# Residual additions and the gates' offset by accumulating DMAs, and the gates' sigmoids three steps later, in a streaming-encoder block on one core

## The chip, the cores and the metric

The kernel runs on one core of a Trainium2 chip. The time is the device time of one execution in microseconds (us); three runs of the kernel before gave a median of 2434.71 us (2432.69 to 2434.84). The core has five engines that each work through their own list of instructions in order: TensorE (PE, with PEld for its weight loads), VectorE (DVE), ScalarE (ACT), GpSimd (POOL) and SyncE (SP), which here issues nearly all DMAs. An engine that comes to an instruction whose inputs are not there waits, and everything behind it in its list waits too.

## The reference

One encoder block on 256 tokens of width 2048, everything in float32: two feed-forward parts with a mixer and a cross attention between them, each added to the scaled residual stream and normalised.

```python
ALPHA = 2.0 ** 0.25
def swiglu_ffn(x, w_in, w_out):                 # width 5504
    g, u = jnp.split(x @ w_in, 2, axis=-1)
    return (jax.nn.silu(g) * u) @ w_out
def hybrid_mixer(u, ...):
    proj = u @ w_in
    qa, ka, va, q_lat, kv_lat, gates = jnp.split(proj, ...)
    y_a = chunked_relbias_attention(...) @ w_o_a
    y_b = mla_attention(...) @ w_o_b
    g = jax.nn.sigmoid(gates + gate_bias)       # 256 x 4096
    g_a, g_b = jnp.split(g, 2, axis=-1)
    return (g_a * y_a + g_b * y_b) @ w_out
h = layer_norm(ALPHA * h + 0.5 * swiglu_ffn(h, ffn1...))
h = layer_norm(ALPHA * h + hybrid_mixer(h, ...))
h = layer_norm(ALPHA * h + memory_cross_attention(h, mem, ...))
h = layer_norm(ALPHA * h + 0.5 * swiglu_ffn(h, ffn2...))
```

## The kernel before

**Weights and the split.** All products have a float32 accuracy that is made of two parts of each operand: a high part hi and a remainder lo. The weights come from memory in chunks of 1 MB (a tile *raw* of 128 x 2048, three buffers), loaded by SyncE (L193), one chunk after the other through the whole kernel. ScalarE copies a chunk into *hi* in two pieces of 128 x 1024 (L264), VectorE subtracts hi from raw and writes *lo* (L267, one instruction of 128 x 2048). TensorE multiplies hi·hi, hi·lo and lo·hi. A chunk covers two blocks of 128 of the inner dimension, for 256 tokens by 1024 output columns: 24 matmuls of 512 columns (`mm_pair`, L311).

**Sums chunks.** For some chunks the product is formed from seven products instead of eight: VectorE makes sums of the weights (`weight_sums`, L248 one instruction of 128 x 1024 and L250 two of 128 x 512) in a tile such as *H*, these are split like a weight (*X* in the rows below), and `mm_sums` (L366) does 21 matmuls. A part of the results is gathered in four PSUM tiles of its own. After the last sums chunk `shared` brings them together: ScalarE copies two (L679, L680), VectorE does four additions (L681 to L684), and the four 128 x 512 tiles in SBUF, `qs["add"]`, in buffers called *w* (six of that kind), hold what is still to be added to the plain product.

**The items.** The program is written as a list of items, about one per chunk (`add`). `collect` builds such a list apart, and `weave` puts side work before given items of it, with a priority. Loads run ahead of the items. A scheduler then makes each engine's list from the order and priorities, so an instruction's place on its engine is not its place in the code.

**Output pairs.** `out_pair` makes 1024 output columns of the residual stream *h* (four tiles of 128 x 512 in two tiles for the tokens). After `shared` its inner function adds `qs["add"]` to h on VectorE: with the factor ALPHA where the pair is the first to touch these columns (L629), else plainly (L631). When all chunks are done, `finish` (L754) adds the PSUM tiles, and the last pairs also feed the statistics of the normalisation (L390). Seven pairs have sums chunks: two and one in each feed-forward part, and one in the cross attention's output (xo). Two pairs of the mixer's output have none, and only use `finish` with the factor.

**Gates.** Four gate groups follow each other, each 1024 columns: `product` adds the four tiles of `qs["add"]` to PSUM (L921), adds the bias (L923), which GpSimd has loaded as a row repeated over the partitions into tile X1 (L912, 512 KB), and takes the sigmoid on ScalarE (L924, two of 128 x 1024 a gate). It is scheduled soon after the gate's last chunk. The results are used only after the attention.

Of the kernel before, what the change touches and what calls it, by code (L numbers as in the profile page):

```python
# [14 lines left out]
ALU = mybir.AluOpType  # L15
# [3 lines left out]
P = 128  # L19
S = 256  # L20
D = 2048
KT = D // P
# [5 lines left out]
SUMS_IN = {2: ("X0", 0), 4: ("X0", 1), 6: None}  # L28
# [3 lines left out]
SUMS_GATE, AT_GATE = {**SUMS_IN, 5: ("F", 0)}, ((2, 4, 5, 6), (2, 4, 5, 6), (2, 4, 6), (2, 4, 6))  # L32
ORDER_GATE = (0, 2, 1, 4, 5, 3, 6, 7)
# [8 lines left out]
SUM_HOME = ("X2", "X3"),  # L42
# [5 lines left out]
ALPHA = 2.0 ** 0.25  # L48
# [53 lines left out]
class Kernel:  # L102
# [513 lines left out]
            turn = None  # L616
            f0 += nf

    def out_pair(self, bank, src, g, nk, x, at, fx, scale, st, sums_in=SUM_HOME):

        nc, h = self.nc, self.h
        ps, qs = {}, {}

        def shared():
            for (tt, a), s in qs["add"].items():
                c = (2 * g + a) * 512
                hs = h[tt][:, c:c + 512]
                if scale:
                    nc.vector.scalar_tensor_tensor(hs, hs, ALPHA, s, ALU.mult, ALU.add)  # L629
                else:  # L630
                    nc.vector.tensor_tensor(hs, hs, s, ALU.add)  # L631

        def finish():
            for tt in range(2):
                for a in range(2):
                    self.finish(tt, 2 * g + a, ps[tt, a], scale and not at, st)
        self.pair_group(bank, src, 512, nk, x, at, fx, ps, qs, shared, sums_in)
        self.add(finish)

    def group_tile(self, j):  # L640
# [229 lines left out]
    def mixer(self, xT, st, steps):  # L870
        nc, t = self.nc, self.t
# [24 lines left out]
        ps = {}  # L896
# [3 lines left out]
        a, b, c = steps(1)  # L900
        self.weave(first, {0: a, 3: b, 4: c})
        gates, fx = {}, {}
# [1 line left out]
        self.weave(second, {1 + i: [self.forms_step(fx, SUMS_GATE, c, xT)] for i, c in enumerate(SUMS_GATE)}, prio=0)  # L904


        bias = {}

        def load_bias(n):
            if "t" not in bias:  # L910
                bias["t"] = self.block("X1", (P, 2, 1024))
            nc.gpsimd.dma_start(bias["t"][:, n % 2, :], t["gate_row"][n:n + 1, :].to_broadcast([P, 1024]))  # L912

        def gate(n):
            ps, qs = {}, {}

            def product():
                g = gates[n] = self.block(f"H{n}", (P, 2, 2, 512))
                for tt in range(2):
                    for a in range(2):  # L920
                        nc.vector.tensor_tensor(g[:, tt, a, :], qs["add"][tt, a], ps[tt, a], ALU.add)  # L921
                    v = g[:, tt].rearrange("p a n -> p (a n)")
                    nc.vector.tensor_tensor(v, v, bias["t"][:, n % 2, :], ALU.add)  # L923
                    nc.scalar.activation(v, v, AF.Sigmoid)  # L924
                if n < 2:
                    load_bias(n + 2)
            self.pair_group(n % 2, t["w_gate"][n], 512, KT, xT, AT_GATE[n], fx, ps, qs, None, SUM_HOME + ("H5",),
                            ORDER_GATE if len(AT_GATE[n]) > 3 else None)
            self.add(product, prio=SOON)

        self.add(lambda: [load_bias(n) for n in range(2)])
        for n in range(4):
            gate(n)


        lps, lqs = {}, {}
# [25 lines left out]
        def lat_send(k):  # L962
            def fn():
                for tt in range(2):
                    with self.tc.issue_after(self.last_load.ins):
                        self.sent = self.send(self.lat[:, tt, k, :], self.lu[:, k, tt, :], 512)
            return fn

        def lat_join(k):
            def fn():  # L970
                if k == 0:
                    self.c = self.act(["X0", "X2"])
                for tt in range(2):
                    self.join(self.lat[:, tt, k, :], self.lu[:, k, tt, :], 512)
                v = self.lu[:, k].rearrange("p t (j c) -> p t j c", j=4)
                for j in range(4):
                    gain = self.vec(("q_a_norm", "kv_a_norm")[k], j)
                    hi, lo = (self.c.at(half, 4 * k + j).rearrange("p (t c) -> p t c", t=2) for half in (0, 1))
                    nc.scalar.mul(hi, v[:, :, j, :], gain)
                    nc.vector.scalar_tensor_tensor(lo, v[:, :, j, :], gain, hi.bitcast(F32), ALU.mult, ALU.subtract)  # L980
            return fn

        self.pair_group(0, t["w_lat"][0], 512, KT, xT, SUMS_IN, fx, lps, lqs, None, SUM_HOME + ("H5",))
        self.add(lat_scale, prio=SOON)
        self.add(lat_planes)

# [225 lines left out]
        for i in range(NA):  # L1212
            side = [[lat_send(0)], [], [lat_join(0)], [lat_join(1)]][2 * i:2 * i + 2] if i < 2 else ([], [])
# [21 lines left out]
        for h in range(B_HEADS):  # L1235
# [18 lines left out]
            if h in (2, 5, 8, 11):  # L1254
                self.add(lambda q=h // 3: self.gb_apply(0, self.h, (q,)), held=held, prio=LATE)
        n = B_HEADS - 1
        ends = {1: [b_out(n - 3), b_send(n), b_out(n - 2)],
                2: [b_join(n - 1), b_out(n - 1)],
                3: [lambda: setattr(self, "early", False), b_join(n), b_out(n)]}
# [52 lines left out]
        main = self.collect(lambda: out_a(0))  # L1312
# [4 lines left out]
        side = out_b(0)  # L1317
        last = {}
        main = self.collect(lambda: last.update(out_b(1)))
# [5 lines left out]
        side = self.mem_norm()  # L1325
# [451 lines left out]
```

## Time and profile before

| | |
|---|---|
| runs | 2434.71 us median (2432.69 to 2434.84) |
| profiled execution | 2432.52 us |
| its span | 2430.7 us |
| DMA engines, mean rate | 212 GB/s |

The prediction shows the profile's rows beside its steps. Three kinds are used. The page's busy line gives each engine's time, its share of the span and its number of instructions. Windows give the same for a stretch of the span. Rows of the chain or of single lines have a start and a duration in us, the engine, the line, the operation, the tile written `<-` the tiles read, the shape, a count where several stand together, and in brackets the idle time before the instruction with what ended it.

### The profile page before, as it was taken

Reading aid. Unit: us, or ns where it says so; the run is one execution under the profiler, and the core shown is the slowest. Engines: PE = TensorE matmul, PEld = TensorE weight load, DVE = VectorE, ACT = ScalarE, POOL = GpSimd, SP = SyncE. Lnnn points to the kernel's source line nnn. Section 1 sums busy time; section 2 is a strip of 40 time slices with the busy share of each in tenths; the row PEclk is TensorE's granted clock in tenths of the full one; section 3 lists DMA queues with packets and bytes.
Section 4 is the critical chain, followed back from the end, with each engine's and each line's share of the span. In section 5 each row is a group of like instructions: output and inputs, shape, how many; then the busy total and the mean of one; then the engine's idle time right before and its main releaser. Section 6 shows DMA issues by size and latency. Waiting matters only on the chain.

```text
span 2430.7 us, 29702 instructions
## 1 busy us (share of the span) xinstructions
PE 2422.3 (100%) x11280; PEld 2022.8 (83%) x11280; DVE 2130.9 (88%) x2437; ACT 1553.2 (64%) x2022; POOL 35.9 (1%) x81
## 2 busy tenths in 40 slices
PE   9999999999999999999999999999999999999999
PEld 8888888888888888888888888888888888888887
DVE  8999989899889998779788889979879999888997
ACT  6676745666555557878565687765666675556662
POOL 0000000000000001000000000000000000000000
PEclk9999999999999999999999999999999999999999
DMA  7766656667656657776577577655556766666665
GB/s 268 252 212 214 207 200 222 210 201 219 224 176 215 216 195 248 229 210 176 183 246 256 167 241 213 220 181 192 190 199 214 229 221 210 220 207 207 200 220 182
DMA packets 176414, 516.20 MB, mean 212 GB/s; under 512 B 111728, under 2 KB 112496, under 8 KB 121104
## 3 DMA queue, kind: packets, MB, share of 16 engines
q1 hardware_dynamic: 170816, 495.83, 61.6%
q0 software_dynamic: 4592, 17.30, 2.2%
q8 instruction: 88, 1.44, 0.2%
q10 hardware_dynamic: 864, 1.18, 0.1%
q14 instruction: 54, 0.44, 0.1%
HBM read 485.30 MB, written 2.10 MB: 201 GB/s over the span
## 4 chain that ended last, share of the span: by engine, by line
PE 89%; DVE 4%; ACT 3%; DMA 1%; issue 1%; SPq 0%; DVEq 0%; ACTq 0%
PE at L311 24%; PE mm L311 23%; PE at L366 11%; PE mm L366 11%; PE mm L298 10%; PE mm L277 4%; PE mm L279 2%; DVE lo L267 2%; ACT hi L264 1%; PE at L1034 1%; PE at L1505 0%; PE at L277 0%; DMA raw<-w_xv 0%; PE at L1088 0%; ACT H L854 0%
## 5 line engine op out<-in xcount | busy, mean ns | idle before, releaser
L264 ACT CAST hi<-raw 128x1024 fp32r<-128x1024 f32 (+1 forms) x852 | 804.0, 981 | 458.0 <-PE at L311 150.1
L267 DVE TENSOR_TENSOR lo<-raw,hi 128x2048 fp32r<-128x2048 f32 (+1 forms) x427 | 902.0, 2114 | 134.8 <-ACT hi L264 129.0
L311 PE MATMUL mm<-hi,T 128*128 128x512 f32 (+1 forms) x1312 | 307.5, 384 | 0.8 <-DVE v L400 0.7
L311 PEld LDWEIGHTS mm<-hi,T 128*128 128x128 f32 x1312 | 244.5, 188 | 46.9 <-DVE v L400 1.1
L264 ACT CAST X<-H 128x1024 fp32r<-128x1024 f32 (+1 forms) x170 | 174.8, 1035 | 160.9 <-DVE H L248 119.9
L311 PE MATMUL at<-hi,T 128*128 128x512 f32 x1136 | 272.3, 390 | 0.0
L311 PEld LDWEIGHTS at<-hi,T 128*128 128x128 f32 x1136 | 213.3, 188 | 44.5
L267 DVE TENSOR_TENSOR X<-H,X 128x2048 fp32r<-128x2048 f32 (+1 forms) x85 | 191.4, 2252 | 64.7 <-ACT X L264 64.7
L311 PE MATMUL mm<-lo,T 128*128 128x512 f32 (+1 forms) x656 | 158.4, 383 | 0.0
L311 PE MATMUL at<-lo,T 128*128 128x512 f32 x568 | 141.0, 389 | 0.0
L311 PEld LDWEIGHTS mm<-lo,T 128*128 128x128 f32 x656 | 122.3, 188 | 22.4
L311 PE MATMUL at<-hi,H 128*128 128x512 f32 x560 | 133.8, 390 | 0.0
L311 PEld LDWEIGHTS at<-lo,T 128*128 128x128 f32 x568 | 106.7, 188 | 22.1
L311 PEld LDWEIGHTS at<-hi,H 128*128 128x128 f32 x560 | 105.0, 188 | 21.5
L250 DVE TENSOR_TENSOR H<-H,raw 128x512 f32<-128x512 f32 (+1 forms) x170 | 115.4, 679 | 2.2
L311 PE MATMUL mm<-hi,H 128*128 128x512 f32 x480 | 115.5, 392 | 0.1
L311 PEld LDWEIGHTS mm<-hi,H 128*128 128x128 f32 x480 | 89.6, 188 | 18.9 <-DVE w L684 0.5
L248 DVE TENSOR_TENSOR H<-raw 128x1024 f32<-128x1024 f32 (+1 forms) x85 | 102.1, 1201 | 0.6 <-DMA raw<-w_gate 0.4
L366 PE MATMUL mm<-X,X 128*128 128x512 f32 x342 | 91.4, 393 | 0.0
L264 ACT CAST X<-raw 128x1024 fp32r<-128x1024 f32 (+1 forms) x54 | 55.4, 1035 | 47.9 <-DVE raw L250 38.6
L366 PE MATMUL at<-X,X 128*128 128x512 f32 (+1 forms) x315 | 82.6, 386 | 0.7 <-ACT X L264 0.7
L854 ACT COPY w<-w 128x1024 uint16<-128x1024 uint16 (+1 forms) x60 | 75.7, 1275 | 1.4 <-DMA w<-w 1.4
(387 smaller groups left out, 4151.3 us busy)
## 6 DMA issues: line engine op xcount, KB each, us to landing
raw<-ffn_w_in SPq DMA_DIRECT2D x150, 1024.0 KB, 4.9
raw<-ffn_w_out SPq DMA_DIRECT2D x66, 1024.0 KB, 4.9
raw<-w_gate SPq DMA_DIRECT2D x32, 1024.0 KB, 4.8
raw<-ffn_w_out_r SPq DMA_DIRECT2D x16, 1024.0 KB, 4.9
raw<-w_qk SPq DMA_DIRECT2D x16, 1024.0 KB, 5.6
raw<-w_o_b SPq DMA_DIRECT2D x16, 1024.0 KB, 4.8
raw<-w_out SPq DMA_DIRECT2D x16, 1024.0 KB, 5.0
raw<-w_xk SPq DMA_DIRECT2D x16, 1024.0 KB, 5.4
```

The costliest lines, as they stand in the source:

```text
L248: self.nc.vector.tensor_tensor(two[0], two[1], raw[:, :m].unsqueeze(1).to_broadcast([P, 2, m]), ALU.add)
L250: self.nc.vector.tensor_tensor(t[:, a * m:a * m + m], t[:, b * m:b * m + m], raw[:, a * m:a * m + m], ALU.add)
L264: self.last_hi = self.nc.scalar.copy(hi[:, c:d], src[:, c:d])
L267: self.last_lo = self.nc.vector.tensor_tensor(lo[:, :n], src, hi[:, :n].bitcast(F32), ALU.subtract)
L277: self.nc.tensor.matmul(ps, hi[j], x.both(kt), start=(j == 0), stop=False)
L279: self.last_mm = self.nc.tensor.matmul(ps[:, :S], lo[j], x.at(0, kt), start=False, stop=(j == n - 1))
L298: self.last_mm = self.nc.tensor.matmul(ps, x.at(xi, kt)[:, tt * P:(tt + 1) * P], w[wi][:, j * 512 + c:j * 512 + c + m], start=(start and j ...
L311: self.last_mm = self.nc.tensor.matmul(ps[tt, g][:, :n], x.at(xi, kt)[:, tt * P:(tt + 1) * P], w[wi][:, c:c + n], start=first and j + wi + ...
L366: self.last_mm = self.nc.tensor.matmul(bank[:, :m], a[xi], v[wi][:, c * m:(c + 1) * m], start=own and first and wi + xi == 0, stop=own and ...
L854: self.nc.scalar.copy(self.words(u, n).rearrange("p (c k) -> p k c", k=2), self.words(s, n).rearrange("p (k c) -> p k c", k=2))
L1034: nc.tensor.matmul(ps[:, c0:c0 + nk], q[:, tt * P:(tt + 1) * P], k[:, :nk], start=(j == 0), stop=(j == len(parts) - 1))
```

## The change

Three edits. In `out_pair` the additions of `qs["add"]` to h become 28 DMAs on GpSimd's queue, 256 KB each, that add to their destination (`accum_op=ALU.add`). Where h needs the factor ALPHA, two ScalarE multiplications of 128 x 1024 (`scaled`) do that beforehand, put in as side work before the third item of the pair. In the gates the bias tile, its four loads and the eight additions go, and eight accumulating DMAs of 512 KB add the bias row, repeated over the partitions, from memory to the gate. The sigmoids become a function of their own, put in as side work before the fourth item of the group that follows (the latents' group for the last gate). Lines behind the edits move by up to three.

```diff
--- before.py
+++ after.py
@@ -616,25 +616,27 @@
             turn = None
             f0 += nf
 
-    def out_pair(self, bank, src, g, nk, x, at, fx, scale, st, sums_in=SUM_HOME):
+    def out_pair(self, bank, src, g, nk, x, at, fx, scale, st, sums_in=SUM_HOME, order=None):
 
         nc, h = self.nc, self.h
         ps, qs = {}, {}
+
+        def scaled():
+            for tt in range(2):
+                hs = h[tt][:, g * 1024:(g + 1) * 1024]
+                nc.scalar.mul(hs, hs, ALPHA)
 
         def shared():
             for (tt, a), s in qs["add"].items():
                 c = (2 * g + a) * 512
-                hs = h[tt][:, c:c + 512]
-                if scale:
-                    nc.vector.scalar_tensor_tensor(hs, hs, ALPHA, s, ALU.mult, ALU.add)
-                else:
-                    nc.vector.tensor_tensor(hs, hs, s, ALU.add)
+                nc.gpsimd.dma_start(h[tt][:, c:c + 512], s, accum_op=ALU.add)
 
         def finish():
             for tt in range(2):
                 for a in range(2):
                     self.finish(tt, 2 * g + a, ps[tt, a], scale and not at, st)
-        self.pair_group(bank, src, 512, nk, x, at, fx, ps, qs, shared, sums_in)
+        main = self.collect(lambda: self.pair_group(bank, src, 512, nk, x, at, fx, ps, qs, shared, sums_in, order))
+        self.weave(main, {2: [scaled]} if scale and at else {}, prio=0)
         self.add(finish)
 
     def group_tile(self, j):
@@ -904,14 +906,7 @@
         self.weave(second, {1 + i: [self.forms_step(fx, SUMS_GATE, c, xT)] for i, c in enumerate(SUMS_GATE)}, prio=0)
 
 
-        bias = {}
-
-        def load_bias(n):
-            if "t" not in bias:
-                bias["t"] = self.block("X1", (P, 2, 1024))
-            nc.gpsimd.dma_start(bias["t"][:, n % 2, :], t["gate_row"][n:n + 1, :].to_broadcast([P, 1024]))
-
-        def gate(n):
+        def gate(n, side):
             ps, qs = {}, {}
 
             def product():
@@ -920,17 +915,22 @@
                     for a in range(2):
                         nc.vector.tensor_tensor(g[:, tt, a, :], qs["add"][tt, a], ps[tt, a], ALU.add)
                     v = g[:, tt].rearrange("p a n -> p (a n)")
-                    nc.vector.tensor_tensor(v, v, bias["t"][:, n % 2, :], ALU.add)
+                    nc.gpsimd.dma_start(v, t["gate_row"][n:n + 1, :].to_broadcast([P, 1024]), accum_op=ALU.add)
+
+            def ends():
+                for tt in range(2):
+                    v = gates[n][:, tt].rearrange("p a n -> p (a n)")
                     nc.scalar.activation(v, v, AF.Sigmoid)
-                if n < 2:
-                    load_bias(n + 2)
-            self.pair_group(n % 2, t["w_gate"][n], 512, KT, xT, AT_GATE[n], fx, ps, qs, None, SUM_HOME + ("H5",),
-                            ORDER_GATE if len(AT_GATE[n]) > 3 else None)
+            main = self.collect(lambda: self.pair_group(
+                n % 2, t["w_gate"][n], 512, KT, xT, AT_GATE[n], fx, ps, qs, None, SUM_HOME + ("H5",),
+                ORDER_GATE if len(AT_GATE[n]) > 3 else None))
+            self.weave(main, side, prio=0)
             self.add(product, prio=SOON)
-
-        self.add(lambda: [load_bias(n) for n in range(2)])
+            return {3: [ends]}
+
+        side = {}
         for n in range(4):
-            gate(n)
+            side = gate(n, side)
 
 
         lps, lqs = {}, {}
@@ -980,7 +980,9 @@
                     nc.vector.scalar_tensor_tensor(lo, v[:, :, j, :], gain, hi.bitcast(F32), ALU.mult, ALU.subtract)
             return fn
 
-        self.pair_group(0, t["w_lat"][0], 512, KT, xT, SUMS_IN, fx, lps, lqs, None, SUM_HOME + ("H5",))
+        main = self.collect(lambda: self.pair_group(
+            0, t["w_lat"][0], 512, KT, xT, SUMS_IN, fx, lps, lqs, None, SUM_HOME + ("H5",)))
+        self.weave(main, side, prio=0)
         self.add(lat_scale, prio=SOON)
         self.add(lat_planes)
 
```

The changes of order at three places follow. The first is ScalarE at the end of gate 1 and the start of gate 2. H_933 (before) and H_932 (after) are gate 1's tile, H_932 and H_931 the tile of gate 2's weight sums, X_940 and X_939 their hi, hi_6209 and hi_6206 the hi of the sums chunk's raw weights, hi_6245 and hi_6242 that of the chunk after. Before:

```order
L680 COPY w_925_6125<-mm_5926 128x512
L264 CAST hi_6160<-raw_6158 128x1024 x2
L264 CAST hi_6209<-raw_6165 128x1024
L924 ACTIVATE H_933_6171<-H_933_6171 128x1024
L264 CAST hi_6209<-raw_6165 128x512
L924 ACTIVATE H_933_6171<-H_933_6171 128x1024
L264 CAST hi_6245<-raw_6243 128x1024
L264 CAST X_940_6214<-H_932_6167 128x1024
L264 CAST hi_6245<-raw_6243 128x1024
```

and of the changed kernel:

```order
L682 COPY w_924_6125<-mm_5924 128x512
L264 CAST hi_6160<-raw_6158 128x1024 x2
L264 CAST X_939_6211<-H_931_6167 128x1024
L264 CAST hi_6206<-raw_6165 128x1024
L264 CAST hi_6206<-raw_6165 128x512
L923 ACTIVATE H_932_6171<-H_932_6171 128x1024 x2
L264 CAST X_939_6211<-H_931_6167 128x1024
L264 CAST hi_6242<-raw_6240 128x1024 x2
```

The two sigmoids now stand together, behind the raw hi and the first half of the sums' hi, and ahead of its second half.

The second place is VectorE in the same stretch: L921 and L923 before, L916 after, write the gate. Before:

```order
L681 TENSOR_TENSOR w_926_6126<-w_924_6124,mm_5927 128x512
L682 TENSOR_TENSOR w_925_6125<-w_925_6125,w_926_6126 128x512
L921 TENSOR_TENSOR H_933_6171<-w_924_6124,at_5884 128x512
L683 TENSOR_TENSOR w_926_6126<-w_926_6126,mm_5928 128x512
L684 TENSOR_TENSOR w_927_6127<-w_925_6125,mm_5928 128x512
L921 TENSOR_TENSOR H_933_6171<-w_925_6125,at_5885 128x512
L921 TENSOR_TENSOR H_933_6171<-w_926_6126,at_5886 128x512
L923 TENSOR_TENSOR H_933_6171<-H_933_6171,X_836_5581 128x1024
L921 TENSOR_TENSOR H_933_6171<-w_927_6127,at_5887 128x512
L267 TENSOR_TENSOR lo_6161<-raw_6158,hi_6160 128x2048
L923 TENSOR_TENSOR H_933_6171<-H_933_6171,X_836_5581 128x1024
L248 TENSOR_TENSOR H_932_6167<-raw_6165 128x1024
```

and of the changed kernel:

```order
L683 TENSOR_TENSOR w_925_6126<-w_923_6124,mm_5925 128x512
L684 TENSOR_TENSOR w_924_6125<-w_924_6125,w_925_6126 128x512
L248 TENSOR_TENSOR H_931_6167<-raw_6165 128x1024
L685 TENSOR_TENSOR w_925_6126<-w_925_6126,mm_5926 128x512
L686 TENSOR_TENSOR w_926_6127<-w_924_6125,mm_5926 128x512
L916 TENSOR_TENSOR H_932_6171<-w_923_6124,at_5882 128x512
L916 TENSOR_TENSOR H_932_6171<-w_924_6125,at_5883 128x512
L916 TENSOR_TENSOR H_932_6171<-w_925_6126,at_5884 128x512
L916 TENSOR_TENSOR H_932_6171<-w_926_6127,at_5885 128x512
L267 TENSOR_TENSOR lo_6161<-raw_6158,hi_6160 128x2048
L250 TENSOR_TENSOR H_931_6167<-H_931_6167,raw_6165 128x512
L267 TENSOR_TENSOR lo_6207<-raw_6165,hi_6206 128x1536
```

The two bias additions are gone, and the first instruction of the next weight sums has moved ahead of the last two additions of `shared` and of the gate.

The third place is VectorE at the end of xo's pair; h_101 and h_102 are the residual stream's two tiles. Before:

```order
L684 TENSOR_TENSOR w_2117_13688<-w_2115_13686,mm_13517 128x512
L629 SCALAR_TENSOR_TENSOR h_101<-h_101,w_2115_13686 128x512
L629 SCALAR_TENSOR_TENSOR h_102<-h_102,w_2116_13687 128x512
L629 SCALAR_TENSOR_TENSOR h_102<-h_102,w_2117_13688 128x512
L267 TENSOR_TENSOR lo_13726<-raw_13723,hi_13725 128x2048
L754 TENSOR_TENSOR h_101<-h_101,at_13336 128x512
L754 TENSOR_TENSOR h_101<-h_101,at_13337 128x512
L390 BN_STATS bn_13731<-h_101 128x6 x2
L754 TENSOR_TENSOR h_102<-h_102,at_13338 128x512
L754 TENSOR_TENSOR h_102<-h_102,at_13339 128x512
```

and of the changed kernel:

```order
L686 TENSOR_TENSOR w_2116_13689<-w_2114_13687,mm_13518 128x512
L756 TENSOR_TENSOR h_101<-h_101,at_13335 128x512
L390 BN_STATS bn_13732<-h_101 128x6
L267 TENSOR_TENSOR lo_13727<-raw_13724,hi_13726 128x2048
L756 TENSOR_TENSOR h_101<-h_101,at_13336 128x512
L756 TENSOR_TENSOR h_102<-h_102,at_13337 128x512
L390 BN_STATS bn_13732<-h_101 128x6
L390 BN_STATS bn_13737<-h_102 128x6
L756 TENSOR_TENSOR h_102<-h_102,at_13338 128x512
L390 BN_STATS bn_13737<-h_102 128x6
```

`finish` (now L756) stands right behind the last addition of `shared`, its first addition ahead of the lo.

## The prediction

> **What bounds the kernel now.** I read the page's busy line and its chain first, then the windows by stage, and then single instructions on either side of the edits.
>
> ```profile
> PE 2422.3 (100%) x11280; PEld 2022.8 (83%) x11280; DVE 2130.9 (88%) x2437; ACT 1553.2 (64%) x2022; POOL 35.9 (1%) x81
> PE 89%; DVE 4%; ACT 3%; DMA 1%; issue 1%; SPq 0%; DVEq 0%; ACTq 0%
> ```
>
> The span is 2430.7 us, so TensorE is without a matmul for 8.4 us in all. A busy PE need not be a fast one, so the rate has to be looked at too, in an undisturbed stretch of the chain and in the stages that the change touches (windows: span, then busy time and count of PE, PEld, DVE, ACT, POOL, clock, DMA share, GB/s):
>
> ```profile
> 1330.12 43.55 PE at L311 x192
> 257.00:319.00 62.00, 62.00 (x276) 51.36 (x275) 57.56 (x58) 38.28 (x45) 0.00 (x0) 1.00 0.65 215
> 740.00:937.00 197.00, 196.97 (x864) 161.43 (x863) 178.41 (x144) 114.71 (x128) 2.50 (x4) 1.00 0.60 208
> 1640.00:1697.00 57.00, 57.00 (x274) 47.77 (x274) 55.20 (x71) 35.68 (x51) 0.00 (x0) 1.00 0.57 202
> 2369.00:2431.00 62.00, 57.28 (x251) 45.52 (x249) 44.51 (x65) 17.58 (x20) 1.27 (x1) 0.98 0.51 178
> ```
>
> 192 matmuls of 512 columns in 43.55 us are 226.8 ns each. The first out pair (257 to 319) runs 276 in 62.00 us, 224.6 ns; the gates (740 to 937) 864 in 197 us, 228.0 ns, which is 864 x 1.2 ns = 1.0 us over the undisturbed rate. In the xo pair PE is never idle. Of the 8.4 idle microseconds 4.7 are behind the last matmul (62.00 - 57.28), where the change has nothing. **So PE is full exactly where VectorE is to be relieved, and about 1 us is all that can be won there.** The question of this case is whether the new waits reach PE.
>
> **What is taken away.**
>
> ```profile
> L629 DVE SCALAR_TENSOR_TENSOR h<-h,w x20: 682/684/693, 307.2 to 2115.0; 128x512 f32<-128x512 f32 x20
> L631 DVE TENSOR_TENSOR h<-h,w x8: 683/685/686, 624.7 to 2366.4; 128x512 f32<-128x512 f32 x8
> L923 DVE TENSOR_TENSOR H<-H,X x8: 1219/1222/1225, 772.3 to 900.9; 128x1024 f32<-128x1024 f32 x8
> L924 ACT ACTIVATE H<-H x8: 1052/1062/1065, 773.6 to 902.1; 128x1024 f32<-128x1024 f32 x8
> ```
>
> VectorE loses 20 x 0.684 + 8 x 0.685 + 8 x 1.222 = 28.9 us of 2130.9. All of it lies beside matmuls, so I credit the path with 0.3 us, a third of the 1.0 us found in the gates, with bounds 0 and 1.0. ScalarE gains 10 multiplications of 128x1024 at the 1.06 us of its sigmoids, 10.6 us. They cost nothing as long as an early hi covers them: in the first pair ScalarE is busy 38.28 of 62 us and, as the rows below show, its hi is 5 us ahead of PE; without that cover each costs at most its 1.06 us. GpSimd gets 36 issues for 4; it is 1% busy, and no product waits for its other work there.
>
> **What is added: waits for landings.** No accumulating DMA stands in this trace. The nearest rows are GpSimd's own loads of the same sizes: 256 KB (gb) and the 512 KB of the very same gate row, with issue to landing as minimum, median and maximum behind them.
>
> ```profile
> w<-gb POOLq DMA_DIRECT2D x24, 256.0 KB, 4.2
> X<-gate_row POOLq DMA_DIRECT2D x4, 512.0 KB, 5.8
> DMA to landing us min/median/max: 3.3/4.2/8.8
> DMA to landing us min/median/max: 5.4/5.8/6.4
> ```
>
> An accumulating DMA also reads its destination. I bound its landing by 3.3 us below and by twice the gate row's median, 11.6 us, above. I take 6.5 us for the 512 KB ones, just over the same-size row's maximum, and 5 us for the 256 KB ones.
>
> The Trainium skill, page "DMA: Bandwidth & Descriptors", section "Anatomy of one DMA — SWDGE (gpsimd) path", gives 2.0 us plus bytes over 436 GB/s, an estimate of 3.2 us for 512 KB. The 5.8 us row is well over that, so the row is used; by the page's figure no sigmoid would wait long enough to matter and the sum would be the 0.3 us credit alone.
>
> **The gates.** The order of ScalarE shows that a sigmoid, although put three steps later in the code, moves past a row or two of hi only. Gate 1 is the tightest. VectorE, ScalarE and PE there, before:
>
> ```profile
> 808.39 2.29 DVE L267 TENSOR_TENSOR lo<-raw,hi 128x2048 fp32r<-128x2048 f32 x1
> 813.78 1.28 DVE L921 TENSOR_TENSOR H<-w,at 128x512 f32<-128x512 f32 x2
> 822.85 1.42 DVE L250 TENSOR_TENSOR H<-H,raw 128x512 f32<-128x512 f32 x2
> 824.46 2.29 DVE L267 TENSOR_TENSOR lo<-raw,hi 128x2048 fp32r<-128x2048 f32 x1 [0.20 <-ACT hi L264]
> 815.99 1.06 ACT L264 CAST hi<-raw 128x1024 fp32r<-128x1024 f32 x1 [3.22 <-PE mm L311]
> 820.16 1.06 ACT L924 ACTIVATE H<-H 128x1024 f32<-128x1024 f32 x1 [1.65 <-DVE H L923]
> 825.56 1.04 ACT L264 CAST X<-H 128x1024 fp32r<-128x1024 f32 x1
> 825.08 1.07 PE L366 MATMUL at<-X,X 128*128 128x512 f32 x4
> ```
>
> In the new order VectorE goes on at 810.6 (end of the lo at 808.39) with two adds of shared, the 1.2 us first half of the sums, two more adds and four L921. Counted at 0.63 us an add (half of the 1.28) the first half of the gate is ready at 815.6 and the second at 816.9; the sums' last part follows by 822. Landing L later, ScalarE does both sigmoids (1.0 us each) and only then the second half of the sums' hi (X, 1.0), and VectorE its lo (2.2). PE begins the sums at 825.08 and, by its new order, wants that second half four matmuls later, at 826.0, and the lo after eight, at 826.9. The second landing is at 816.9 + L, the sigmoid ends 1.0 later, X 1.0 later, lo 2.2 later: 821.1 + L. **PE loses L - 5.8 us.** What queues behind a waiting sigmoid is thus hi, lo, and PE in turn. In gates 2 and 3 the X stands between the two sigmoids, so only the first landing counts (1.3 us earlier): PE loses L - 7.1 us each. Gate 0 has a whole chunk more in front and begins to lose at about 10.5 us. At 6.5 us that is 0.7 + 0 + 0 + 0 = 0.7 us; at 5.8 nothing; at 8.8, 3.0 + 2 x 1.7 = 6.4; at 11.6, 5.8 + 2 x 4.5 + 1.1 = 15.9.
>
> **The out pairs.** finish (L754) now waits for landings instead of following the additions. VectorE and PE in the first pair of ffn1, and in the pair of xo, where only one chunk lies between:
>
> ```profile
> 312.52 0.68 DVE L684 TENSOR_TENSOR w<-w,at 128x512 f32<-128x512 f32 x1
> 318.71 1.28 DVE L754 TENSOR_TENSOR h<-h,mm 128x512 f32<-128x512 f32 x2 [1.51 <-PE mm L311]
> 328.26 1.98 PE L311 MATMUL at<-lo,H 128*128 128x512 f32 x8
> 305.68 1.05 ACT L264 CAST hi<-raw 128x1024 fp32r<-128x1024 f32 x1 [1.69 <-DMA raw<-ffn_w_out]
> 312.14 2.00 ACT L264 CAST hi<-raw 128x1024 fp32r<-128x1024 f32 x2 [3.50 <-PE mm L311]
> 319.19 3.79 PE L311 MATMUL at<-hi,H 128*128 128x512 f32 x16
> 1694.28 0.69 DVE L682 TENSOR_TENSOR w<-w,w 128x512 f32<-128x512 f32 x1
> 1695.61 0.68 DVE L684 TENSOR_TENSOR w<-w,mm 128x512 f32<-128x512 f32 x1
> 1704.99 2.27 DVE L267 TENSOR_TENSOR lo<-raw,hi 128x2048 fp32r<-128x2048 f32 x1
> 1709.58 1.07 PE L298 MATMUL mm<-lo,X 128*128 128x512 f32 x4
> ```
>
> In ffn1 the last sum is ready at 313.2 and finish comes at 318.7, 5.5 us later; what stands behind it is a lo that PE wants at 328.26, so landings up to some 12 us cost PE nothing. The second pair's finish is later still, and ffn2 repeats both. In xo the last sum is ready at about 1695.7 (0.6 earlier without the addition at its head); the four additions (2.5 us) are gone, but the fourth finish waits for 1695.7 + L. At 5 us that is 1700.7, before VectorE gets there, and the lo of 1704.99 comes no later than now. At 8.8 us it ends at about 1709.1, still ahead of 1709.58; at 11.6 PE loses some 2 us.
>
> **Sum.** -0.3 + 0.7 + 0 = +0.4 us on the profiled 2432.52 (span 2430.7 and 1.8 around it), 2432.9. The median of the runs shown, 2434.71, is 2.2 above that execution, so the forecast is 2432.9 + 2.2 = 2435.1 us, no change that can be told. A measurement of this kernel can tell about 0.2%, 4.9 us, from none.
>
> **Rivals.**
> 1. *Slow landings.* If the accumulation makes a 512 KB landing 8.8 to 11.6 us, the sigmoids hold ScalarE, and the sums above give 6.4 to 15.9 + 2 = 17.9 us more; at 10 us it is 4.2 + 2 x 2.9 = 10.0 in place of 0.7, giving 2444.4. It decides against the forecast from L = 8.4, where the gates' 2.6 + 2 x 1.3 = 5.2 us pass 4.9. For it: nothing in this trace adds to a destination, and gb had one landing of 8.8. Against it: the gate row's four lie within 5.4 to 6.4. Chance 17%.
> 2. *The accumulations crowd the weight loads.* In the first pair the DMA engines are 0.65 busy for 215 GB/s, 331 at full share. Four DMAs of 256 KB with their destinations read are 2.1 MB, 6.3 us of all engines in one burst. The hi at 305.68 already waited 1.69 us for its load, so a late load is a late hi; that of 312.14 ends 5.1 us before PE wants it at 319.19. A load 6.3 us late would cost 1.2 us in each of seven pairs, 8.4 us: 2443.5. Against it: two thirds of the engines' time is taken, one third free, and the burst is spread over 6 us by VectorE. The Trainium skill, same page, section "Issuing engines are not separate DMA queues", speaks against the change here: GpSimd's transfers run on the same engines as SP's. That the engines are shared the trace can show only for loads: theirs spread as the row below has it, with no accumulation among them. Chance 5%.
>
> ```profile
> DMA to landing us min/median/max: 3.4/4.9/9.7
> ```
>
> 3. *VectorE's relief reaches PE elsewhere.* The order of many chunks shifts a little; if waits outside these stages went, 3.7 us of idle PE before the tail (8.4 - 4.7) and 1 us of slow rate would be the most: 2435.1 - 4.7 = 2430.4. Chance 5%, and hardly beyond 0.2%.
> 4. *The change does not do what it says.* The scaling is hoisted to ffn1's third group and the sigmoids move by a row or two: the landing wait is then the whole effect, which is the forecast's 0.7 us or rival 1.
>
> **How the numbers follow.** The forecast, landings up to 7.5 us, has 73%. The range runs from 2431.5 (credit 1.0, no loss, and a median 2 us lower by chance) to 2446, which takes in rival 2 and most of rival 1; some 8% lie above and 6% below. Faster by over 0.2%: 4%, the end of rival 3. Slower: rival 1's 17% and most of rival 2, 21%. Same: 75%.
>
> **What would show it.** PE at 100% and 226.8 ns in the same stages, with VectorE down by about 29 us and ScalarE up by 10.6, shows the first step. Landings of the new DMAs near 6.5 and 5 us, ScalarE waiting for them at the sigmoids by a few microseconds with no hole on PE at the sums' chunks of gates 1 to 3, shows the second; holes there of L - 5.8 would show the sum right and the landing wrong. A finish that waits for a DMA while lo arrives in time shows the third. I am wrong if PE gets holes at the out pairs, if the weight loads land later there, or if the time falls by more than 5 us.

## The result and the profile after

The changed kernel took 2446.45 us in the median (2444.79 to 2451.94, 5 runs), the kernel before 2434.84 us (2432.69 to 2435.88, 5 runs) on the same chip: 11.6 us more, a ratio of 1.0053 with a 95% interval of 1.0042 to 1.0064. The forecast was 2435.1 us with a range up to 2446, so the time lies 0.45 us above the range.

The busy line and the chain of the changed kernel's page:

```profile
PE 2426.3 (99%) x11280; PEld 2021.7 (83%) x11280; DVE 2107.3 (86%) x2401; ACT 1561.1 (64%) x2032; POOL 65.1 (3%) x113
PE 75%; issue 8%; DVE 7%; DMA 4%; ACT 4%; SPq 0%; POOL 0%; DVEq 0%; ACTq 0%; POOLq 0%
```

VectorE is busy for 23.6 us less (2130.9 to 2107.3; the removed instructions were 28.9), ScalarE for 7.9 us more, and neither helps TensorE: the span grew by 15.7 us (2430.7 to 2446.4), and TensorE, which was idle for 8.4 us, now is for 20.1. VectorE, DMAs and ScalarE have come into the chain. Two stages hold most of the new idle time, the gates and the second half of the cross attention's output. The windows of these two stages in the changed kernel (span, then busy time and count of PE, PEld, DVE, ACT, POOL, clock, DMA share, GB/s):

```profile
741.00:944.00 203.00, 198.60 (x867) 161.71 (x866) 170.43 (x136) 115.11 (x128) 8.41 (x10) 1.00 0.67 220
1640.00:1760.00 120.00, 117.17 (x537) 96.74 (x536) 102.30 (x125) 69.37 (x92) 3.53 (x4) 0.99 0.63 213
```

TensorE stands for 203.00 - 198.60 = 4.4 us at the gates and for 2.8 us around the xo pair, where it stood for 0.03 and 0 before. The holes are not the whole loss at the gates: it did 867 matmuls in these 203 us, the kernel before 890, and 23 matmuls are 5.2 us at 0.227 each. What it waits for is seen in the order of time. ScalarE at the end of gate 1 in the changed kernel (start, duration, instruction, idle time before it and its releaser), and behind it TensorE:

```profile
819.04 1.57 ACT L264 CAST hi<-raw 128x1024 fp32r<-128x1024 f32 x2 [2.52 <-issue]
822.10 1.06 ACT L923 ACTIVATE H<-H 128x1024 f32<-128x1024 f32 x1 [1.49 <-DMA H<-gate_row]
828.36 1.06 ACT L923 ACTIVATE H<-H 128x1024 f32<-128x1024 f32 x1 [5.20 <-DMA H<-gate_row]
829.32 1.03 ACT L264 CAST X<-H 128x1024 fp32r<-128x1024 f32 x1
...
828.09 1.07 PE L366 MATMUL at<-X,X 128*128 128x512 f32 x4
830.40 0.74 PE L366 MATMUL at<-X,X 128*128 128x512 f32 x2 [1.25 <-ACT X L264]
...
832.73 0.96 PE L366 MATMUL at<-X,X 128*128 128x512 f32 x3 [1.11 <-DVE X L267]
```

This is the chain that the prediction's gate paragraph worked out, link by link: the second sigmoid waits 5.20 us for its landing, the second half of the sums' hi (X) starts only behind it at 829.32, TensorE wants it after four matmuls and waits 1.25 us, and then 1.11 us more for VectorE's lo of the same sums. What differs is the landing. The DMAs of this gate, and of all four gates, issue to landing:

```profile
L918 POOL DMA_DIRECT2D H<-gate_row x2: 863/864/866, 817.2 to 818.4; - x2
DMA to landing us min/median/max: 4.8/7.4/9.9
...
L918 POOL DMA_DIRECT2D H<-gate_row x8: 863/863/871, 773.9 to 906.5; - x8
DMA to landing us min/median/max: 4.8/7.5/9.9
```

The first accumulation of a gate lands after 4.8 to 5.2 us, the second, issued 1.2 us later, after 9.8 to 9.9, in every gate. The forecast had 6.5 us for each.

The changed kernel's profiled execution (2448.21 us) is 1.8 us above its median, and that of before 2.3 below, which is why the two spans lie 15.7 us apart and the medians 11.6. A part of that is a wait for weight loads ahead of the normalisation behind the first feed-forward part, where TensorE's hole was 1.6 us in this profile; in those of the experiments below it lay between nothing and 2.6 us (0.8 in E7, whose pairs have no DMAs), so it is not counted.

### The profile page after: what moved, and what is told of

Its sections match the earlier page's. It is cut to its first block, busy times and chain, and to the rows that moved or that the text cites. A ratio compares the mean times of both kernels' runs of the same rounds, so it can differ in the third digit from the quotient of the medians.

```text
span 2446.4 us, 29787 instructions
## 1 busy us (share of the span) xinstructions
PE 2426.3 (99%) x11280; PEld 2021.7 (83%) x11280; DVE 2107.3 (86%) x2401; ACT 1561.1 (64%) x2032; POOL 65.1 (3%) x113
## 3 DMA queue, kind: packets, MB, share of 16 engines
q0 software_dynamic: 9200, 26.74, 4.6%
## 4 chain that ended last, share of the span: by engine, by line
PE 75%; issue 8%; DVE 7%; DMA 4%; ACT 4%; SPq 0%; POOL 0%; DVEq 0%; ACTq 0%; POOLq 0%
PE at L311 23%; PE mm L311 20%; PE mm L366 9%; PE at L366 9%; PE mm L298 5%; PE mm L277 4%; DVE lo L267 3%; PE mm L279 2%; ACT hi L264 2%; PE at L1036 1%; DMA raw<-w_xq 1%; ACT X L264 1%; DMA raw<-w_gate 1%; PE at L1507 0%; PE at L277 0%
## 5 line engine op out<-in xcount | busy, mean ns | idle before, releaser
L366 PEld LDWEIGHTS mm<-X,X 128*128 128x128 f32 x342 | 63.7, 188 | 15.1 <-DVE X L267 2.1
```

The source lines that it names most:

```text
L366: self.last_mm = self.nc.tensor.matmul(bank[:, :m], a[xi], v[wi][:, c * m:(c + 1) * m], start=own and first and wi + xi == 0, stop=own and ...
```

## The experiments

All ratios are to the kernel before on the same chip in the same series.

### Which part costs

E1 has the change in the gates alone (`out_pair` as before), E2 in the output pairs alone (gates as before). The diff of each is the corresponding part of the change's diff.

> Only the gates' part of the change; the output pairs add on VectorE as before. Theory A (the landings: ScalarE stands at the second sigmoid of a gate until the second 512 KB accumulation lands about 10 us after its issue, and the hi behind it is late for TensorE): the gates lose what the trace of the changed kernel shows there, 4.4 us of idle TensorE between 740 and 937, so about 2439.5 us, and nothing is lost at the xo pair or at the normalisation behind it. Theory B (the accumulations crowd the weight loads): the gates carry 4 of the 11 MB that are added, so about a third of the 11.6 us, 2438.5, and it shows as late weight loads, not as waits for the gate row. Theory C (only the instructions' new order costs): the same 2439 but no wait of ScalarE for a landing before TensorE's holes.

> Only the output pairs' part; the gates as before. Theory A: the additions of finish wait for the 256 KB landings (8 us in the changed kernel); in ffn1 and ffn2 something else covers that, in xo the lo behind them is late, a weight buffer comes free late, and 3 to 4.5 us are lost at the normalisation behind xo: 2438 to 2440 us. Theory B: each of the seven pairs loses a part, and the time is 2441 to 2443, the holes spread over ffn1 and ffn2 too.

E1 took 2441.70 us against 2433.82 (ratio 1.0034, 1.0021 to 1.0046), 7.9 us more; E2 2438.56 (1.0023, 1.0013 to 1.0032), 4.7 us more. Together that is 12.6 us, about the whole loss of 11.6. Windows of E1 and of E2 over the gates and the xo pair:

```profile
741.00:940.00 199.00, 191.85 (x832) 156.58 (x831) 164.45 (x129) 109.40 (x122) 7.14 (x8) 0.99 0.65 211
1640.00:1760.00 120.00, 120.00 (x561) 100.07 (x560) 108.61 (x140) 71.28 (x94) 0.00 (x0) 1.00 0.58 204
```

```profile
741.00:940.00 199.00, 198.97 (x872) 162.83 (x871) 181.49 (x147) 116.82 (x134) 3.72 (x9) 1.00 0.60 210
1640.00:1760.00 120.00, 115.87 (x543) 96.00 (x542) 101.64 (x134) 67.27 (x91) 3.52 (x4) 1.00 0.60 202
```

With the gates' part alone TensorE stands for 7.2 us at the gates and not at all at xo; with the pairs' part alone it is full at the gates and stands for 4.1 us at xo. Theory A had the places right and the gates' size too low (2439.5 expected); the second landing was 11.6 us at gate 1 in this run. Theory B's holes at all seven pairs are not there.

### The landing, the place, or the traffic at the gates

E3 adds the bias on VectorE again, from the loaded tile, and keeps the sigmoids as side work three steps later:

```diff
-                    nc.gpsimd.dma_start(v, t["gate_row"][n:n + 1, :].to_broadcast([P, 1024]), accum_op=ALU.add)
+                    nc.vector.tensor_tensor(v, v, bias["t"][:, n % 2, :], ALU.add)
+                if n < 2:
+                    load_bias(n + 2)
...
```

> The changed kernel with the bias added by VectorE from a loaded tile again, and the sigmoids still three steps later. Theory A: without the landings the sigmoids wait for nothing; the gates' 4.4 us go, about 2442 us, TensorE full between 740 and 937. Theory C (the place of the sigmoids and the new order cost, not the landing): as the changed kernel, 2446.

E4 keeps the DMAs and pins the sigmoids behind the next chunk's hi. It takes such a tie, because the number of the step alone does not move them: with step 4 or 6 in place of 3 the scheduler leaves all eight sigmoids at the same places of ScalarE's list.

```diff
-                    nc.scalar.activation(v, v, AF.Sigmoid)
+                    with self.tc.issue_after(self.next_hi.ins):
+                        nc.scalar.activation(v, v, AF.Sigmoid)
...
-            return {3: [ends]}
+            return {4: [ends]}
```

> The changed kernel with its accumulating DMAs, but each pair of sigmoids is held behind the hi of the chunk after the one now behind it (put before the fifth item of the next group and issued after the next chunk's hi), some 12 us after the DMAs. Theory A: the landings are over by then, so ScalarE does not wait there, TensorE has no holes at the gates and about 2442 us are left. Theory B: the DMAs still run at the same time beside the same loads, so it stays at 2446.

E3 took 2437.68 us (1.0015, 1.0006 to 1.0024) and E4 2437.20 (1.0014, 1.0005 to 1.0022), against 2433.82: they stand 3.9 and 3.4 us over the kernel before, where the whole change stands 11.6 over its own, so both give back about 8 us. That is E1's 7.9, and more than the 4.4 us of holes at the gates that the expectations went by. So it is not the sigmoids' later step by itself (E3 has it, and TensorE is busy for 198.97 of the gates' 199 us), and not the transfers (E4 has them). E3 does not settle the new order: with the additions back, VectorE's list at gate 1 is that of the kernel before, and the first half of the sums' hi stands behind the sigmoids. E8 below has the change's order of both engines there. E4 shows that the transfers cost nothing by themselves. The gates' window, the two accumulations of gate 1, and the two weight loads issued right behind them; and, in a second fence, the window and the two loads at the same place in the kernel before:

```profile
741.00:940.00 199.00, 199.00 (x878) 164.46 (x878) 173.92 (x139) 117.34 (x136) 9.63 (x15) 1.00 0.69 228
...
L918 POOL DMA_DIRECT2D H<-gate_row x2: 863/863/863, 813.5 to 814.7; - x2
DMA to landing us min/median/max: 5.1/8.2/11.3
...
L193 SPq DMA_DIRECT2D raw<-w_gate x2: 328/328/328, 816.7 to 819.7; - x2
DMA to landing us min/median/max: 8.8/9.2/9.5
```

```profile
741.00:940.00 199.00, 198.97 (x873) 163.05 (x872) 181.35 (x147) 116.71 (x134) 2.84 (x6) 1.00 0.60 210
...
L193 SPq DMA_DIRECT2D raw<-w_gate x2: 328/328/328, 810.7 to 819.0; - x2
DMA to landing us min/median/max: 4.7/4.9/5.0
```

The loads beside the accumulations land after 9 us in place of 5, as rival 2 had it, and TensorE does not miss them: it is busy for 199.00 of 199.00 us and gets through 878 matmuls where the kernel before did 873. The late loads are covered; the waiting sigmoid was not.

### What makes the second landing late

E8 lets all 36 DMAs write in place of adding; the gates are then the sigmoid of the bias row alone, and the residual stream keeps only the last part.

```diff
-                nc.gpsimd.dma_start(h[tt][:, c:c + 512], s, accum_op=ALU.add)
+                nc.gpsimd.dma_start(h[tt][:, c:c + 512], s)
...
-                    nc.gpsimd.dma_start(v, t["gate_row"][n:n + 1, :].to_broadcast([P, 1024]), accum_op=ALU.add)
+                    nc.gpsimd.dma_start(v, t["gate_row"][n:n + 1, :].to_broadcast([P, 1024]))
```

> The changed kernel with all 36 DMAs writing their destination instead of adding to it, so the gates are the sigmoid of the bias row alone and the residual stream holds the last part only: a measure of what the accumulation costs. If the addition is the price, the 512 KB rows land like the loads of the same row before, 5.4 to 6.4 us, the second of a gate too, and the gates' holes shrink to below 1.5 us. If it is the queue or the size, the second lands after about 10 us again and the time stays near 2446.

It was executed once, in 2435.96 us. Its windows over the gates and the xo pair, and the eight DMAs at the gates with their landings:

```profile
741.00:940.00 199.00, 199.00 (x879) 164.40 (x878) 173.33 (x139) 117.76 (x135) 6.32 (x14) 1.00 0.64 229
1640.00:1760.00 120.00, 119.74 (x565) 99.57 (x564) 105.11 (x144) 70.74 (x98) 2.15 (x4) 1.00 0.60 209
...
L918 POOL DMA_DIRECT2D H<-gate_row x8: 530/530/536, 772.7 to 897.7; - x8
DMA to landing us min/median/max: 3.6/4.3/5.9
```

The addition is the price. The same rows written plainly at the same places land after 3.6 to 5.9 us, the second of a gate too, and TensorE has no hole at the gates, though ScalarE and VectorE have the change's order at gate 1. The pages' rows of GpSimd's queue fit: its 26.74 MB took 4.6% of the DMA engines' time in the changed kernel and 3.3% here, and the 17.30 MB of the kernel before took 2.2%. By these shares the 36 DMAs held the engines about twice as long when they added, an estimate.

E11 leaves one accumulation a gate and adds the second bias on VectorE:

```diff
-                    nc.gpsimd.dma_start(v, t["gate_row"][n:n + 1, :].to_broadcast([P, 1024]), accum_op=ALU.add)
+                    if tt == 0:
+                        nc.gpsimd.dma_start(v, t["gate_row"][n:n + 1, :].to_broadcast([P, 1024]), accum_op=ALU.add)
+                    else:
+                        nc.vector.tensor_tensor(v, v, bias["t"][:, n % 2, :], ALU.add)
...
```

> The changed kernel with only the first of a gate's two biases added by DMA, the second by VectorE from a loaded tile; the sigmoids stand together behind the raw hi and, in gate 1, ahead of the second half of the sums' hi, as in the change. Theory A in its exact form (the second accumulation waits in the queue behind the first; one alone lands in 5 us, under the 5.8 us from which the prediction's sum loses): the gates' holes shrink from 4.4 us to under 1 us and about 2438 us are left, the xo pair's part. If one alone lands in 8 us or more, or if the wait for any landing costs, the holes stay at 3 to 4 us and the time is 2443 or more.

It took 2438.99 us against 2433.57 (1.0017, 1.0008 to 1.0026). Its gates' window and its four accumulations:

```profile
741.00:940.00 199.00, 198.88 (x875) 163.52 (x874) 177.13 (x143) 116.38 (x134) 7.31 (x13) 1.00 0.66 222
...
L926 POOL DMA_DIRECT2D H<-gate_row x4: 862/874/884, 771.8 to 896.1; - x4
DMA to landing us min/median/max: 4.8/4.9/5.1
```

An accumulation alone lands after 4.8 to 5.1 us, below the 5.8 us from which the prediction's sum begins to lose, and the hole is 0.1 us. ScalarE still waits 4.5 us in all for these landings; TensorE does not notice. The loss at the gates is in the second accumulation: issued 1.2 us after the first, it landed 6.3 us after it in gate 1 of the changed kernel (822.0 and 828.3). E11 stands 5.4 us over its kernel before, 2.0 us more than E4 does; no trace places these 2 us at the gates.

### The xo pair: the wait or the traffic

In E4 only the pairs' loss was left. VectorE at the xo pair in E4, with TensorE's wait behind it:

```profile
1696.62 0.69 DVE L756 TENSOR_TENSOR h<-h,at 128x512 f32<-128x512 f32 x1 [0.58 <-DMA h<-w]
...
1702.72 0.69 DVE L756 TENSOR_TENSOR h<-h,at 128x512 f32<-128x512 f32 x1 [2.49 <-DMA h<-w]
1704.27 0.69 DVE L756 TENSOR_TENSOR h<-h,at 128x512 f32<-128x512 f32 x1 [0.86 <-DMA h<-w]
...
1707.79 0.69 DVE L756 TENSOR_TENSOR h<-h,at 128x512 f32<-128x512 f32 x1 [1.64 <-DMA h<-w]
...
1709.12 2.27 DVE L267 TENSOR_TENSOR lo<-raw,hi 128x2048 fp32r<-128x2048 f32 x1
...
1707.41 1.98 PE L298 MATMUL mm<-hi,X 128*128 128x512 f32 x8
1711.45 1.20 PE L298 MATMUL mm<-lo,X 128*128 128x512 f32 x4 [2.07 <-DVE lo L267]
```

VectorE waits 5.6 us in four pieces for the landings, the lo behind them starts at 1709.12, and TensorE waits 2.07 us for it. The last of the four landed after 11.4 us. In the changed kernel the landings there were 7.6 to 9.0 us, and TensorE had no hole at this lo; its hole came 40 us on, at the normalisation, where VectorE had arrived late:

```profile
1742.12 2.29 DVE L267 TENSOR_TENSOR lo<-raw,hi 128x2048 fp32r<-128x2048 f32 x1 [3.03 <-ACT hi L264]
1744.49 2.29 DVE L267 TENSOR_TENSOR X<-raw,X 128x2048 fp32r<-128x2048 f32 x1
...
1735.60 6.83 DMA raw<-ffn_gate
...
1742.45 2.01 ACT L264 CAST X<-raw 128x1024 fp32r<-128x1024 f32 x2 [0.36 <-DMA raw<-ffn_gate]
...
PE at L421 <- DVE h L413: 2.7, 1, 2.7
```

Between the two lies a chain: a late lo frees its raw tile late, the load into it starts late, and so the next hi and lo. The last links of it are the load at 1735.60, ScalarE's cast of it (X, at 1742.45) and VectorE's X at 1744.49, which stands ahead of the normalisation; the lo before it had waited 3.03 us for a hi from the load before. The last row is TensorE's only wait of this stage in the view of waits (us in total, times, longest): 2.7 us for the normalised h.

E5 is E4 with xo alone back on VectorE, without the two multiplications on ScalarE there; E9 is E5 with four accumulating DMAs at the same place into a tile that nobody reads (the lines that clear this tile and that drop the multiplications are left out below).

```diff
-                nc.gpsimd.dma_start(h[tt][:, c:c + 512], s, accum_op=ALU.add)
+                hs = h[tt][:, c:c + 512]
+                if scale and st is not None:
+                    nc.vector.scalar_tensor_tensor(hs, hs, ALPHA, s, ALU.mult, ALU.add)
+                    i = 2 * tt + a                                                       # E9 alone
+                    nc.gpsimd.dma_start(scr["t"][:, i * 512:(i + 1) * 512], s, accum_op=ALU.add)   # E9 alone
+                else:
+                    nc.gpsimd.dma_start(hs, s, accum_op=ALU.add)
...
```

> The kernel with the sigmoids behind the next chunk's hi, and in it the xo pair alone adds on VectorE as before the change (the factor ALPHA too); the six feed-forward pairs keep their accumulating DMAs. Theory A (what is left there, 3.4 us in the runs' medians, is the wait of xo's finish for its landings): it goes, 2433 to 2434 us, about the kernel before, and TensorE is full from 1640 to 1760. Theory B (any burst of accumulating DMAs costs a part): only a seventh goes, about 2436.5.

> As the kernel whose xo pair adds on VectorE (2433.7 us), and besides that four accumulating DMAs of 256 KB at the same place, from the same tiles into a tile that nobody reads, cleared beforehand by GpSimd; VectorE's order is the same, and nothing waits for these DMAs. If the crowding of the weight loads costs at xo (theory B), two loads there land 2 to 3 us later, as with the change, and the time is 2436 to 2437, TensorE with holes of 3 us from 1640 to 1760. If only the wait of finish costs (theory A), the loads land late too but the time stays at 2433.7.

E5 took 2433.73 us against 2433.55 (1.0001, 0.9992 to 1.0010), E9 2434.77 against 2434.16 (0.9999, 0.9990 to 1.0008): both the time of the kernel before. E9's window around xo, its four idle accumulations and the weight loads beside them, and the loads there in the kernel before:

```profile
1640.00:1760.00 120.00, 120.00 (x568) 100.22 (x567) 108.26 (x151) 72.69 (x101) 5.36 (x5) 1.00 0.60 208
...
L642 POOL DMA_DIRECT2D X<-w x4: 870/969/1321, 1691.6 to 1697.9; - x4
DMA to landing us min/median/max: 7.5/8.2/11.4
...
L193 SPq DMA_DIRECT2D raw<-w_xo_r x3: 327/328/328, 1692.3 to 1701.6; - x3
DMA to landing us min/median/max: 7.5/7.7/9.1
```

```profile
L193 SPq DMA_DIRECT2D raw<-w_xo_r x3: 328/328/328, 1691.0 to 1700.3; - x3
DMA to landing us min/median/max: 4.6/6.5/6.7
```

The loads land 1 to 3 us later beside the accumulations, and TensorE is busy for all of the 120 us. So with VectorE's order of before the crowding alone costs nothing here either; the loss needs VectorE's wait in `finish`, with what it hands on. The change's order at xo and the multiplications on ScalarE are not the cause: E8 has both, and with its landings of 5.3 to 7.1 us there TensorE is busy for 119.74 of the 120 us. What the wait would cost without the late loads was not tested; in the changed kernel the load behind the first late lo, issued at 1711.38, took 7.5 us, where its counterpart before took 4.6.

E6 and E10 keep xo's DMAs and put `finish` later, two chunks and one:

```diff
...
+        pair = self.collect(pair_items)
+        fin = pair.pop()[0]
+        def finish():
+            with self.tc.issue_after(self.last_lo.ins):
+                fin()
+        self.weave(pair + self.collect(proj_items), {1: [out(2), out(3), form(2)], 2: [form(4)], 4: [form(6)],
+                                                     len(pair) + 2: [finish]}, prio=0)      # E10: + 1
```

> The kernel with the sigmoids behind the next chunk's hi, and xo's additions by DMA as in the change, but its finish is put two chunks later and behind four or five lo, about 11 us after the last DMA's issue. Theory A: the landing is over when VectorE comes there, the loss at xo goes as with VectorE's additions, 2433 to 2434 us, or up to 1 us better. If the transfers themselves delay TensorE (theory B), it stays at 2437.

> The kernel with the sigmoids behind the next chunk's hi; xo's finish by DMA's result is put one chunk later instead of two, behind two lo, where VectorE stood idle for 4 us in the run with two chunks. Theory A with a collision (the additions that were moved two chunks fell among the last lo ahead of the normalisation): the last landing comes about when VectorE gets there, and the time is 2434 to 2435. Theory B: the late load of the xo weights remains, 2437 to 2438.

E6 took 2438.09 us against 2433.55 (1.0020, 1.0011 to 1.0029): no gain, though VectorE no longer waits in `finish`. Theory A as written there failed. Its profile shows why in part: the additions and statistics now stand as 5 us without a gap ahead of the last weights' lo, just before the normalisation, and TensorE's hole of 3 us is there:

```profile
1721.64 1.28 DVE L756 TENSOR_TENSOR h<-h,at 128x512 f32<-128x512 f32 x2
...
1725.22 1.27 DVE L390 BATCH_NORM_STATS2 bn<-h 128x6 f32<-128x512 f32 x2
1726.42 2.27 DVE L267 TENSOR_TENSOR H<-raw,H 128x2048 fp32r<-128x2048 f32 x1
```

E10, one chunk earlier, took 2435.22 us against 2434.16 (1.0003, 0.9994 to 1.0012), some 2 us better than E4 beside their own runs of before. Its profiled execution, at 2438.06 us the slowest of the eleven, still has the hole at the normalisation, though VectorE neither waits in `finish` there nor has the additions just ahead of the normalisation:

```profile
1709.82 2.00 ACT L264 CAST T<-raw 128x1024 fp32r<-128x1024 f32 x2 [4.98 <-DMA raw<-w_xo_r]
...
PE at L421 <- DVE h L413: 2.4, 1, 2.4
```

ScalarE waits 4.98 us there for a weight load that took 8.9 us beside the accumulations; E6 had one of 8.3 us at the same place. So the collision in E6 is argued, not shown: late loads (theory B) can cost once `finish` stands later, and no trace shows how E10's faster executions got by.

### The part that is worth keeping

E7, and E12 with the same kernel again, has the gates' DMAs, the sigmoids behind the next chunk's hi, and the output pairs as before.

> Only the gates' part, with the sigmoids behind the next chunk's hi; no output pair uses a DMA. Theory A: no loss is left and VectorE's relief of 8 x 1.22 us at the gates shows as 0.5 to 1.3 us, about 2433 us against 2433.8 of the kernel before.

> The gates' part alone with the sigmoids behind the next chunk's hi, which came out at 2431.4 us against 2433.55 of the kernel before with an interval of 0.9984 to 1.0002: a second set of runs. If VectorE's relief at the gates is worth the 1 us that was read from the profile of before, the ratio is again 0.9990 to 0.9996; if it was chance, 1.0000.

E7 took 2431.40 us against 2433.55 (0.9993, 0.9984 to 1.0002), E12 2431.49 against 2433.57 (0.9991, 0.9983 to 1.0000). Both medians are 2.1 us below the kernel before, in two series, while both intervals still reach it. At the gates TensorE did 879 matmuls in 199 us, where before it did 873: 6 x 0.227 = 1.4 us. Whether the rest is real stays open. E5, which differs from E7 in the six feed-forward pairs alone, is 2.3 us above it in the same series. Their intervals, which are to the kernel before, overlap, but nine of E5's eleven executions are slower than the slowest of E7's, so these pairs' DMAs seem to cost some 2 us too. The profiles do not show how: in E5's TensorE waits 1.5 us in all for the last addition of `shared`, in E7's 0.3, and none of these waits is at a feed-forward output pair.

## Why the prediction was wrong

**What bounds the kernel** was right: TensorE is full, and VectorE's relief is worth about 1 us. E4 and E7 show 1.1 to 1.4 us of it in the gates once the waits are out of the way; the forecast credited 0.3, with 1.0 as the upper bound.

**The failed step** is in "What is added: waits for landings": "I take 6.5 us for the 512 KB ones, just over the same-size row's maximum, and 5 us for the 256 KB ones." A 512 KB accumulation alone lands after 4.8 to 5.1 us (E11), so one of them would have been below the estimate. But a gate issues two, 1.2 us apart, and the second lands after 9.8 to 11.6 us, behind the first; a plain write in its place takes at most 5.9 (E8). The nearest row, the four bias loads, held no accumulation. Two of them had been issued 0.7 us apart and landed after 5.9 and 6.4 us, so the row gave no sign of what a pair of accumulations costs, and the estimate gave each the time of a single one. The same holds for the 256 KB ones: 6.0 to 10.7 us with a median of 8.0 in the changed kernel, 7.6 to 9.0 at xo.

**The gates' sum** stood with the right landing put in. It says that gate 1 loses L - 5.8 us from the second landing, gates 2 and 3 only from the first. At 9.9 us that is 4.1 for gate 1; the trace shows 1.25 + 1.11 = 2.4. The gate's last addition ended at 818.1 in place of the 816.9 in the working, and TensorE came to the sums at 828.09, 3.0 us later than before, because earlier holes had already delayed it: 4.1 + 1.2 - 3.0 = 2.3. E1 agrees: 5.8 us at its 11.6, 0.6 less for the earlier addition and 1.3 less for the later TensorE are 3.9, and its two waits are 2.9 and 1.1. Gate 0, which was to lose only from 10.5 us, lost 0.5 us at 9.9 and 0.9 a chunk later; the cover of "a whole chunk more" was overrated. Behind the DMAs of gates 2 and 3 TensorE has no wait in the view, as the sum says for a first landing of 5 us. The hole of 0.6 us at 861.70 lies ahead of gate 2's DMAs: TensorE waits for the last addition of `shared`, which the new order puts behind the next weight sums, and these had waited 1.3 us for their load. The sum has no such term. E11 confirms the threshold from below, at 4.9 us no loss to speak of.

**The out pairs** were forecast at nothing, and xo's stage lost 2.2 to 4.7 us of TensorE in the profiles with xo as in the change (E11 and E4 are the ends). A part of that is the landing again: the text had "at 11.6 PE loses some 2 us", and E4, at 11.4, shows 2.07. The rest was left out of the steps. The working followed one lo to the one matmul that wants it, and took a lo that comes in time as harmless. In the changed kernel it came in time, and handed its lateness on through raw tile, load and hi to the normalisation. The six ffn pairs seem to cost some 2 us (E5 against E7), where the forecast had nothing; no hole of TensorE stands at them.

**Rival 1** (slow landings) is what happened, at the 10 us point for the second DMA: it gave 2444.4 us, measured were 2446.45. It had 17%, for it asked whether one landing is slow, and the evidence against it, four landings within 5.4 to 6.4 us, was of loads that do not add. **Rival 2** was right about the traffic, loads of 7.3 to 9.5 us beside the gates' accumulations, and wrong about its cost at the gates (E4) and at xo in the order of before (E9); E10's profile shows that it can cost in another order. **Rival 3** looked for a gain outside these stages; the gain that E7's profile shows is in the gates. **Rival 4** was right in its first half: the sigmoids' new step alone does not take them out of the way.

## What to carry to other kernels

Where an engine's work is replaced by DMAs that come in pairs, price the last landing of the burst, not one transfer, and ask what stands in the queue behind the instruction that waits for it. The change took 28.9 us from an engine that was not the bottleneck: the gates' 9.8 of them were worth 1 to 2 us, for the pairs' 19.2 no run shows a gain, and the whole change cost 11.6. A consumer of an asynchronous result may have to be tied behind the next work of its engine: here a later step in the program left the sigmoids at the same places of ScalarE's list, and the tie moved them.

## What the runs showed of the hardware

Two accumulating DMAs of 512 KB on GpSimd's queue, issued 1.2 us apart, landed after 4.8 to 5.2 and 9.8 to 9.9 us in the changed kernel, the second after up to 11.6 us in E1; the same two as plain writes after 3.6 to 4.1 and 4.6 to 5.9 us (E8). 256 KB added from one SBUF tile to another took longer (median 8.0 us, with four in a burst) than 512 KB added from a row in memory alone (4.9 us, E11). The issue of a 512 KB accumulation kept GpSimd for 0.86 us, that of a plain write for 0.53. Weight loads of 1 MB in flight beside the gates' accumulations landed after 7.3 to 9.5 us (changed kernel and E4), at gate 1 of the kernel before after 4.7 to 5.5; in E4's gates TensorE was busy throughout all the same.
